# The first attention's TensorE order: written out by hand as a pipeline over heads, with the projections cut in three

## The chip, the cores and the metric

The kernel runs on one core of one Trainium2 chip. The metric is the device time of one execution, in microseconds. All weights are read from the chip's HBM during the run; the activations of the 256 tokens stay in the core's SBUF.

## What is computed

A trunk of two layers over 256 tokens of width 2048 (SEQ = 256, DEPTH = 2). Layer 0's token mixer is a sparse attention with 32 heads; only this part is touched by the change. Cut to what matters:

```python
def dsa_attention(h, w_in, ..., w_qb, w_idx_qb, w_uk, w_uv, w_out, rel_bias):
    q_lat, c_kv, k_idx, w_idx = jnp.split(h @ w_in, ...)         # 512, 256, 128, 16 columns, normalised
    q = (q_lat @ w_qb).reshape(B, S, 32, 128)
    ...
    score = jnp.einsum('bqsh,bqh->bqs', jax.nn.relu(dots), wb)   # 16 indexer heads
    _, idx = lax.top_k(score, 64)                                # which keys a token may see
    logits = (q . w_uk . kv_sel) * 128 ** -0.5 + rel_bias[bucket]
    probs = softmax(logits)
    out = (probs . kv_sel . w_uv)                                # 32 heads of 128
    return out @ w_out
```

The top 64 keys are expressed as a mask over all 256 keys. Layer 1's mixer is a stick-breaking attention, and each mixer is followed by an MLP of 8192 hidden columns; these stages follow the touched one and are the same in both kernels.

## The kernel before

**Split products.** Weights are fetched as fp32 (`raw`, 128x1024, a ring of 4 buffers, loads issued by SP in order) and each is split into a high part (`whi`, ScalarE, L128) and a low part (`wlo`, VectorE, L129), rings of 4 buffers each. A product is then three matmuls (high with high, high with low, low with high: `mm3` L123 to L125, `m_piece` L353 to L355).

**The first attention** works on groups of four heads, `hq` from 0 to 7. `a_project(hq)` makes the group's queries (`pqT`, 48 matmuls of 256 columns), keys (`pkT`, 24) and values (`pv`, 12 of 512 columns), from one unit of query weights (two `raw`) and one `raw` each for keys and values. `a_attend(hq, hl)` handles one head: logits `lg` (L776) with the mask added (L779); a softmax on VectorE (L784, L786, L791) and ScalarE (exp L789, scaling L794); three transposes `pT` (L797), which ScalarE copies to SBUF (L799); the values' product `av` (L802, L803); and a split of its result into `o`. `a_out(hq, d)` multiplies a group's four heads with one of four blocks of `a_w_out` (`m`, 24 matmuls of 512 columns), added into `y` on VectorE.

**The mask.** VectorE finds the 64 largest scores by eight rounds of maximum and replacement (L829, L830) for each half of the tokens, GpSimd cuts the causal part (L833), TensorE transposes the result (`mt`, L839).

**The filler.** At fixed points (`filler.tick`) VectorE adds rows of the conditioning weights (`adaw`, L205) for later stages; a finished gate is spread over the partitions by two small matmuls per quarter (`gate`, L244, L245), with a split `ahl` (L128, L129) in between.

**What sets the order.** The kernel is written as a program and a scheduler reorders the instructions of each engine by readiness and program order, with cost estimates of its own. So in the kernel before, TensorE's order in the attention is the scheduler's, made from this loop: 

```python
for hq in range(8):
    ready, projected = projected, a_project(hq + 1) if hq < 7 else None
    for hl in range(4):
        a_attend(hq, hl, *ready)
        if hq > 0:
            a_out(hq - 1, hl)
```

Each engine executes its own order strictly one after another, and an instruction that waits holds up all behind it.

Of the kernel before, what the change touches and what calls it, by code (L numbers as in the profile page):

```python
# [12 lines left out]
AF = mybir.ActivationFunctionType  # L13
# [3 lines left out]
P = 128  # L17
# [16 lines left out]
BLK = 512  # L34
NB = D // BLK
# [8 lines left out]
def trunk(ctx: ExitStack, tc: tile.TileContext, x, c, rel_bias, ada_w, ada_b, norm_g, a_w_in, a_q_norm,  # L44
          a_kv_norm, a_idx_k_norm, a_w_qb, a_w_idx_qb, a_w_uk, a_w_uv, a_w_out, b_w_in, b_w_out,
          mlp_w1, mlp_w2, bucket, out):
    nc = tc.nc
# [71 lines left out]
    def rows(w, k0, k1, c0, c1):  # L119
        return w.rearrange("(a p) n -> p a n", p=P)[:, k0:k1, c0:c1]  # L120
# [27 lines left out]
    def bank(kind, name):  # L148
        ring = rings[kind]
        ring[1] += 1  # L150
        return psum.tile([P, BLK], F32, tag=f"bank{ring[0][(ring[1] - 1) % len(ring[0])]}", name=uid(name))

    def small_ps(name, tag="s"):
        return bank(tag, name)
# [174 lines left out]
    def unit(src, a, n, weight=1, into=None):  # L329
        if prepared:  # L330
            return prepared.pop()
        r = halves(fetch(src, a, n), a, n, into)
        filler.tick(weight)
        return r
# [148 lines left out]
    def pair_tile(i, name):  # L483

        return arena.tile([P, 2, 2, T], F32R, tag=f"slot{i}", name=uid(name))
# [99 lines left out]
    outs = ((pq, BLK, 0), (pk, W2, BLK))  # L585
    waiting = []
    for i in range(len(steps) + LEAD):
        if i < len(steps):
            start_load(i)
            g, k, _ = steps[i]  # L590
# [134 lines left out]

    def a_project(hq):

        qparts = unit(rows(a_w_qb[0], 0, 4, hq * BLK, (hq + 1) * BLK), 4, BLK)
        khi, klo = a_kv_unit(uk_src, hq)
        vhi, vlo = a_kv_unit(uv_src, hq)  # L730
        qk = []
        for a in range(2):
            pf = bank("f", "pqT")
            s_piece([(k, hi[:, a * 2 * P:(a + 1) * 2 * P], lo[:, a * 2 * P:(a + 1) * 2 * P])
                     for k, (hi, lo) in enumerate(qparts)], q_of, 2, [pf], 4)
            qT = q_tile[:, hq % 2, a].rearrange("p (a t) -> p a t", a=2)
            nc.scalar.activation(qT, pf.rearrange("p (a t) -> p a t", a=2), AF.Copy, scale=QS)
            pf = bank("f", "pkT")
            for b in range(2):
                for k in range(2):  # L740
                    xh, xl = kv_of(k)
                    h = a * 2 + b
                    mm3(pf[:, b * T:(b + 1) * T], khi[:, h, k * P:(k + 1) * P], klo[:, h, k * P:(k + 1) * P],
                        xh, xl, start=(b == 0 and k == 0), stop=(k == 1))
            kT = k_tile[:, hq % 2, a].rearrange("p (a t) -> p a t", a=2)
            nc.scalar.activation(kT, pf.rearrange("p (a t) -> p a t", a=2), AF.Copy)
            qk.append((qT, kT))
        vt = []
        pv = [bank("m", "pv") for _ in range(NT)]
        vu = [(k, vhi[:, :, k * P:(k + 1) * P], vlo[:, :, k * P:(k + 1) * P]) for k in range(2)]  # L750
        m_piece(vu, kv_of, [p_.rearrange("p (h d) -> p h d", h=4) for p_ in pv], 2)
        for t in range(NT):
            v = v_tile[:, hq % 2, t]
            nc.scalar.activation(v, pv[t], AF.Copy)  # L754
            vt.append(v)
        return qk, vt

    biases, o_tile = {}, {}

    def a_attend(hq, hl, qk, vt):  # L760

        a, b = divmod(hl, 2)
        qT, kT = qk[a]
        if hl == 0:
            biases[0] = arena.tile([P, 2, 2, T], F32, tag=f"slot{12 + hq % 2}", name=uid("bias"))
        if b == 0:
            nc.gpsimd.dma_start(out=biases[0][:, a], in_=bass.AP(tensor=tab_d.tensor,
                                                                 offset=tab_d.offset + (4 * hq + hl) * 3 * P,
                                                                 ap=[[1, P], [3 * P, 2], [1, T]]))
            o_tile[0] = pair_tile((11, 16, 17, 18, 10)[(2 * hq + a) % 5], "o")  # L770
        bias = biases[0][:, a]
        ps = small_ps("lg", "lg")
        kw = dict(skip_group_check=True)
        for t in range(NT):
            f, ks = krng[t]
            nc.tensor.matmul(ps[:, f], qT[:, b, t * P:(t + 1) * P], kT[:, b, ks], start=(t == 0), stop=False, **kw)  # L776
        for i in range(3):
            f = slice(i * P, (i + 1) * P)
            nc.tensor.matmul(ps[:, f], mask_t[:, f], big_flip, start=False, stop=(i == 2), **kw)  # L779
        lg = lg_tile[:, hl % 2, :3 * P]  # L780
        st = small.tile([P, 6], F32, tag="st", name=uid("st"))
        for t in range(NT):
            f, _ = krng[t]
            nc.vector.tensor_tensor_reduce(lg[:, f], ps[:, f], bias[:, b, :(t + 1) * P], 1.0, -3.4e38,  # L784
                                           ALU.add, ALU.max, st[:, t:t + 1])
        nc.vector.tensor_scalar(st[:, 2:4], st[:, 0:2], -1.0, None, op0=ALU.mult)  # L786
        for t in range(NT):
            f, _ = krng[t]
            nc.scalar.activation(lg[:, f], lg[:, f], AF.Exp, bias=st[:, 2 + t:3 + t], accum_out=st[:, 4 + t:5 + t])  # L789
        rc = small.tile([P, 2], F32, tag="rc", name=uid("rc"))  # L790
        nc.vector.reciprocal(rc, st[:, 4:6])  # L791
        for t in range(NT):
            f, _ = krng[t]
            nc.scalar.activation(lg[:, f], lg[:, f], AF.Copy, scale=rc[:, t:t + 1])  # L794
        ps = small_ps("pT")
        for i, j in enumerate((0, 2, 1)):
            nc.tensor.transpose(ps[:, i * P:(i + 1) * P], lg[:, j * P:(j + 1) * P], ident)  # L797
        pT = pT_tile[:, hl % 2, :3 * P]
        nc.scalar.activation(pT, ps[:, :3 * P], AF.Copy)  # L799
        ps = small_ps("av", "av")  # L800
        hs = slice(hl * P, (hl + 1) * P)
        nc.tensor.matmul(ps[:, :T], vt[1][:, hs], pT[:, :T], start=True, stop=False, **kw)  # L802
        nc.tensor.matmul(ps[:, P:T], vt[0][:, hs], pT[:, T:], start=False, stop=True, **kw)  # L803
        o = o_tile[0][:, b]
        split(o[:, 0], o[:, 1], ps[:, :T])
        o_tiles[hq].append(o)
        filler.tick(0.33)

    def a_kv_unit(src, hq):
        raw = raw_tile()  # L810
        nc.sync.dma_start(out=raw.rearrange("p (h n) -> p h n", h=4), in_=src[:, 4 * hq:4 * hq + 4, :])
        hi, lo = part_tiles()
        split(hi, lo, raw)
        filler.tick(0.5)
        return hi.rearrange("p (h n) -> p h n", h=4), lo.rearrange("p (h n) -> p h n", h=4)
# [1 line left out]
    def o_of(tiles):  # L817
        return lambda k: (tiles[k][:, 0], tiles[k][:, 1])

    projected = a_project(0)  # L820

    for s in (slice(0, P), slice(2 * P, 3 * P)):
        nc.gpsimd.affine_select(out=score[:, s], in_=score[:, s], pattern=[[-1, P]], compare_op=ALU.is_ge,
# [22 lines left out]
        out_part(a_w_out[0], 4 * q, 4, o_of(o_tiles[q]), yt, gates.get((0, 2)), ss, d, q == 0, q == 7,  # L846
                 ("x", "f", "m")[-len(d):], **kw)

    for hq in range(8):
        ready, projected = projected, a_project(hq + 1) if hq < 7 else None  # L850
        for hl in range(4):
            a_attend(hq, hl, *ready)
            if hq > 0:
                a_out(hq - 1, hl)
    filler.finish()
    a_out(7, 0)
    early = {}
# [256 lines left out]
```

## Time and profile before

| what | value |
|---|---|
| median of 3 runs | 2447.61 us (2441.55 to 2448.34) |
| the profiled execution | 2444.33 us |
| its span, first to last instruction | 2442.5 us |
| TensorE (PE) busy | 2350.5 us, 96% |
| VectorE (DVE) busy | 1747.2 us, 72% |
| ScalarE (ACT) busy | 1222.3 us, 50% |
| mean granted TensorE clock | 0.988 |
| first q product of the attention, last `av` | 177.1 us, 508.99 us |

The difference between the execution's time and its span, 1.8 us, lies ahead of the first and behind the last instruction. Busy time of PE is the union of the records of its matmuls, whose ends are modelled; PEld are the weight loads, which overlap with matmuls. A released wait is shown as idle time and the name of what ended it.

### The profile page before, as it was taken

The page shows a single profiled execution, that of the slowest core. Times are in us where ns is not written, and L with a number is a line of the kernel's source. Part 1 is how long each engine was busy: PE and PEld are TensorE (multiplying, and loading weights), DVE is VectorE, ACT ScalarE, POOL GpSimd, SP SyncE. Part 2 cuts the span into 40 slices and gives each one's busy share as a digit, 9 for nine tenths or more (in the row PEclk, how much of TensorE's full clock was granted, in tenths as well). Part 3 has the DMA queues.
Part 4 walks back from the last instruction along what each step waited for, and adds up shares of the span by engine and source line. Part 5 has one row for each costly group of instructions (what it writes and reads, how often), then busy time and mean ns, then how long its engine had stood idle before and what let it go on. Part 6 is the DMA issues. An engine that isn't in the chain of part 4 may idle for free.

```text
span 2442.5 us, 32827 instructions
## 1 busy us (share of the span) xinstructions
PE 2350.5 (96%) x12292; PEld 1957.9 (80%) x12292; DVE 1747.2 (72%) x2218; ACT 1222.3 (50%) x1825; POOL 41.0 (2%) x74
## 2 busy tenths in 40 slices
PE   5789999999999999999999999999999999999998
PEld 2478887868888888888878989987788888888886
DVE  6789798888576876876567678887855557655556
ACT  3056555566544544444455554456654454454443
POOL 0010000000000000000000000000000000000000
PEclk9799999999999999999999999999999999999999
DMA  9986789857677877877657779896666557656554
GB/s 371 346 311 233 267 307 309 292 206 267 232 261 246 293 269 274 303 253 272 193 186 257 239 264 328 304 335 221 235 239 191 185 188 263 216 189 190 182 189 146
DMA packets 281831, 613.93 MB, mean 251 GB/s; under 512 B 19668, under 2 KB 36392, under 8 KB 281160
## 3 DMA queue, kind: packets, MB, share of 16 engines
q1 hardware_dynamic: 278544, 603.14, 71.8%
q0 software_dynamic: 2464, 8.53, 1.2%
q8 instruction: 96, 1.57, 0.3%
q14 instruction: 63, 0.52, 0.1%
q10 hardware_dynamic: 664, 0.17, 0.0%
HBM read 609.62 MB, written 2.15 MB: 250 GB/s over the span
## 4 chain that ended last, share of the span: by engine, by line
PE 78%; DMA 7%; DVE 5%; ACT 4%; issue 4%; POOL 0%; SPq 0%; DVEq 0%; POOLq 0%; ACTq 0%
PE f L884 18%; PE m L355 11%; PE m L354 11%; PE m L353 11%; PE f L886 9%; DVE acc L205 2%; DMA raw<-in_a_w_out_dram 2%; DMA w<-in_ada_w_dram 2%; DMA adaw<-in_ada_w_dram 1%; ACT whi L128 1%; PE pv L353 1%; PE pv L354 1%; PE pv L355 1%; DVE wlo L129 1%; PE pq L123 1%
## 5 line engine op out<-in xcount | busy, mean ns | idle before, releaser
L129 DVE TENSOR_TENSOR wlo<-raw,whi 128x1024 fp32r<-128x1024 f32 x726 | 875.5, 1220 | 424.6 <-ACT whi L128 421.5
L128 ACT ACTIVATE whi<-raw 128x1024 fp32r<-128x1024 f32 x726 | 756.0, 1056 | 806.9 <-PE f L884 311.2
L884 PE MATMUL f<-h,whi 128*128 128x512 f32 x1920 | 675.9, 394 | 0.0
L886 PE MATMUL f<-h,wlo 128*128 128x256 f32 x1920 | 543.2, 283 | 0.2 <-DVE wlo L129 0.2
L884 PEld LDWEIGHTS f<-h,whi 128*128 128x128 f32 x1920 | 360.6, 188 | 82.5
L205 DVE SCALAR_TENSOR_TENSOR acc<-adaw,cs,acc 128x1024 f32<-128x1024 f32 x300 | 384.1, 1280 | 53.1 <-DMA adaw<-in_ada_w_dram 49.8
L353 PE MATMUL m<-whi,hid 128*128 128x512 f32 x1016 | 401.4, 395 | 0.0
L355 PE MATMUL m<-wlo,hid 128*128 128x512 f32 x1016 | 400.9, 395 | 0.0
L354 PE MATMUL m<-whi,hid 128*128 128x512 f32 x1016 | 400.9, 395 | 0.0
L886 PEld LDWEIGHTS f<-h,wlo 128*128 128x128 f32 x1920 | 360.9, 188 | 1.9 <-DVE wlo L129 0.8
L355 PEld LDWEIGHTS m<-wlo,hid 128*128 128x128 f32 x1016 | 191.3, 188 | 44.7
L353 PEld LDWEIGHTS m<-whi,hid 128*128 128x128 f32 x1016 | 191.4, 188 | 44.0
L354 PEld LDWEIGHTS m<-whi,hid 128*128 128x128 f32 x1016 | 191.4, 188 | 43.3
L387 DVE TENSOR_TENSOR y<-m,y 128x512 f32<-128x512 f32 x200 | 136.7, 685 | 38.4 <-PE m L355 38.0
L353 PE MATMUL m<-whi,o 128*128 128x512 f32 x368 | 149.8, 407 | 0.0
L355 PE MATMUL m<-wlo,o 128*128 128x512 f32 x368 | 146.5, 400 | 0.4 <-DVE wlo L129 0.4
L354 PE MATMUL m<-whi,o 128*128 128x512 f32 x368 | 146.8, 399 | 0.0
L205 DVE SCALAR_TENSOR_TENSOR acc<-w,cs,acc 128x1024 f32<-128x1024 f32 (+1 forms) x74 | 79.6, 1075 | 11.1 <-DMA w<-in_ada_w_dram 8.9
L355 PEld LDWEIGHTS m<-wlo,o 128*128 128x128 f32 x368 | 69.4, 189 | 15.6 <-DVE wlo L129 1.0
L353 PEld LDWEIGHTS m<-whi,o 128*128 128x128 f32 x368 | 69.6, 189 | 13.6 <-ACT qkv L754 0.2
L354 PEld LDWEIGHTS m<-whi,o 128*128 128x128 f32 x368 | 69.6, 189 | 13.3
L123 PE MATMUL pk<-h,whi 128*128 128x256 f32 x256 | 72.8, 284 | 0.0
(274 smaller groups left out, 2912.9 us busy)
## 6 DMA issues: line engine op xcount, KB each, us to landing
raw<-in_mlp_w_dram SPq DMA_DIRECT2D x504, 512.0 KB, 4.5
adaw<-in_ada_w_dram SPq DMA_DIRECT2D x320, 512.0 KB, 6.3
raw<-in_b_w_in_dram SPq DMA_DIRECT2D x92, 512.0 KB, 5.2
raw<-in_a_w_out_dram SPq DMA_DIRECT2D x64, 512.0 KB, 5.6
w<-in_ada_w_dram SPq DMA_DIRECT2D x62, 512.0 KB, 10.3
raw<-in_b_w_out_dram SPq DMA_DIRECT2D x32, 512.0 KB, 6.9
raw<-in_a_w_qb_dram SPq DMA_DIRECT2D x16, 512.0 KB, 5.9
win<-in_a_w_in_dram SPq DMA_DIRECT2D x3, 1824.0 KB, 12.0
```

Of the source, the lines that this page charges most:

```text
L123: nc.tensor.matmul(o, sh, mh, start=start, stop=False, skip_group_check=True)
L128: return (nc.scalar.activation(dst_hi, src, AF.Copy).ins, nc.vector.tensor_sub(dst_lo, src, dst_hi.bitcast(F32)).ins)
L129: nc.vector.tensor_sub(dst_lo, src, dst_hi.bitcast(F32)).ins)
L205: nc.vector.scalar_tensor_tensor(acc, w, cs[:, k:k + 1], acc, op0=ALU.mult, op1=ALU.add)
L353: nc.tensor.matmul(o, xh[:, ts_], hi, start=(k == 0), stop=False)
L354: nc.tensor.matmul(o, xl[:, ts_], hi, start=False, stop=False)
L355: nc.tensor.matmul(o, xh[:, ts_], lo, start=False, stop=(k == n - 1))
L387: nc.vector.tensor_add(y, pt[d][t], y)
L884: nc.tensor.matmul(pf[f], hi[:, fs], hb.rearrange("p a t -> p (a t)"), start=(u == 0 and i == 0), stop=False, skip_group_check=True)
L886: nc.tensor.matmul(pf[f][:, :T], lo[:, fs], hb[:, 0], start=False, stop=(u == 3 and i == 3), skip_group_check=True)
```

## The change

`a_project` becomes a generator in three parts, queries, keys, values, and each part fetches and splits its weights only when it is reached (before, all splits of a group stood at its head, and queries and keys were made in two halves). `a_attend` becomes a generator in three parts: logits with softmax, transposes with their copy, `av` with the split. Around both, `tc.manual_schedule` for TensorE alone keeps TensorE's instructions in the order in which the program writes them; the other engines' orders are still the scheduler's. The new loop writes, for each step, the logits of one head, one `m` block of the group before, the transposes of the previous head, the next part of a projection, and the previous head's `av`. Every engine executes the same instructions as before, in another order.

```diff
     def a_project(hq):
 
-        qparts = unit(rows(a_w_qb[0], 0, 4, hq * BLK, (hq + 1) * BLK), 4, BLK)
+        both = lambda pf: pf.rearrange("p (a t) -> p a t", a=2)
+        qk, vt = ([], []), []
+        parts = unit(rows(a_w_qb[0], 0, 4, hq * BLK, (hq + 1) * BLK), 4, BLK)
+        pf = [bank("f", "pqT") for _ in range(2)]
+        s_piece([(k, hi, lo) for k, (hi, lo) in enumerate(parts)], q_of, 4, pf, 4)
+        for a in range(2):
+            qk[0].append(both(q_tile[:, hq % 2, a]))
+            nc.scalar.activation(qk[0][a], both(pf[a]), AF.Copy, scale=QS)
+        yield
         khi, klo = a_kv_unit(uk_src, hq)
-        vhi, vlo = a_kv_unit(uv_src, hq)
-        qk = []
         for a in range(2):
-            pf = bank("f", "pqT")
-            s_piece([(k, hi[:, a * 2 * P:(a + 1) * 2 * P], lo[:, a * 2 * P:(a + 1) * 2 * P])
-                     for k, (hi, lo) in enumerate(qparts)], q_of, 2, [pf], 4)
...
             pf = bank("f", "pkT")
...
+        yield
+        vhi, vlo = a_kv_unit(uv_src, hq)
         pv = [bank("m", "pv") for _ in range(NT)]
...
-        return qk, vt
+        projected[hq] = list(zip(*qk)), vt
...
-    def a_attend(hq, hl, qk, vt):
+    def a_attend(hq, hl):
+
+        qk, vt = projected[hq]
...
             nc.scalar.activation(lg[:, f], lg[:, f], AF.Copy, scale=rc[:, t:t + 1])
+        yield
         ps = small_ps("pT")
...
         nc.scalar.activation(pT, ps[:, :3 * P], AF.Copy)
+        yield
         ps = small_ps("av", "av")
...
-    projected = a_project(0)
+    projected = {}
+    attention_order = ExitStack()
+    attention_order.enter_context(tc.manual_schedule(engines={mybir.EngineType.PE}))
+    for _ in a_project(0):
+        pass
+    project = a_project(1)
+    next(project)
...
-    for hq in range(8):
-        ready, projected = projected, a_project(hq + 1) if hq < 7 else None
-        for hl in range(4):
-            a_attend(hq, hl, *ready)
-            if hq > 0:
-                a_out(hq - 1, hl)
+    heads = [divmod(h, 4) for h in range(32)]
+    outs = []
+    before = None
+    for hq, hl in heads + [(8, 0)]:
+        now = a_attend(hq, hl) if hq < 8 else None
+        if now:
+            next(now)
+        if outs:
+            a_out(*outs.pop(0))
+        if before:
+            next(before)
+        next(project, None)
+        if before:
+            next(before, None)
+        if hl == 0 and hq > 0:
+            outs += [(hq - 1, d) for d in range(NB)] if hq < 8 else []
+        if hl == 3:
+            for _ in project:
+                pass
+            project = a_project(hq + 2) if hq < 6 else iter(())
+        before = now
+    for o_ in outs:
+        a_out(*o_)
+    attention_order.close()
     filler.finish()
     a_out(7, 0)
```

The lines of the touched functions move: the transposes are L798 in the changed kernel and L797 before, their copy L800 and L799, `av` L804 and L805 for L802 and L803, `mt` L849 for L839, the maxima L839 for L829.

TensorE at the mask. In the kernel before, `mt` stands behind the projections of groups 0 and 1 (`pv_1463` is the last of group 1), the first logits of two heads and the first of group 2's keys (`pkT_1662`):

```order
L355 MATMUL pv_1463<-wlo_1372,ckv_638 128x512
L776 MATMUL lg_1481<-qkv_636,qkv_635 128x128
L776 MATMUL lg_1481<-qkv_636,qkv_635 128x256
L776 MATMUL lg_1514<-qkv_636,qkv_635 128x128
L776 MATMUL lg_1514<-qkv_636,qkv_635 128x256
L123 MATMUL pqT_1636<-qlat,whi_1607 128x256
...
L123 MATMUL pkT_1662<-ckv_638,whi_1620 128x256
L839 LDWEIGHTS misc
L839 MATMUL mt_1316<-ident_b,misc 128x128
```

In the changed kernel it stands right behind the queries of group 1 (`pqT_1281`), and the first head's logits, a gate and the keys of group 1 (`pkT_1441`) follow it:

```order
L123 MATMUL pqT_1281<-qlat,whi_1265 128x256
L124 MATMUL pqT_1281<-qlat,whi_1265 128x256
L125 MATMUL pqT_1281<-qlat,wlo_1266 128x256
L849 LDWEIGHTS misc
L849 MATMUL mt_1393<-ident_b,misc 128x128
...
L776 MATMUL lg_1410<-qkv_636,qkv_635 128x128
L776 MATMUL lg_1410<-qkv_636,qkv_635 128x256
L779 LDWEIGHTS misc
L779 MATMUL lg_1410<-big_flip,misc 128x128
...
L244 MATMUL gate_1434<-ahl_1277,ones_r 128x256
L245 MATMUL gate_1434<-ahl_1277,ones_r 128x256
L123 MATMUL pkT_1441<-ckv_638,whi_1428 128x256
```

Keys, values and the second group's first logits moved from ahead of the mask to behind it.

TensorE between a head's transposes and its `av`. Before, the transposes (`pT_2632`) are interleaved with an output block (`m_2661`) and the next head's logits (`lg_2688`):

```order
L797 MATMUL pT_2632<-ident,lg_640 128x128
L353 MATMUL m_2661<-whi_2650,o_2333 128x512
L797 MATMUL pT_2632<-ident,lg_640 128x128 x2
L354 MATMUL m_2661<-whi_2650,o_2333 128x512
L355 MATMUL m_2661<-wlo_2651,o_2333 128x512
L776 MATMUL lg_2688<-qkv_636,qkv_635 128x128
L802 MATMUL av_2637<-lg_641,qkv_637 128x256
```

In the changed kernel, in the last step of a group (here the third head of group 2, in the step of the fourth head's logits), an output block ends, the transposes follow it, and `av` follows them:

```order
L353 MATMUL m_2386<-whi_2375,o_1971 128x512
L354 MATMUL m_2386<-whi_2375,o_1971 128x512
L355 MATMUL m_2386<-wlo_2376,o_1971 128x512
L798 MATMUL pT_2413<-ident,lg_640 128x128 x3
L804 MATMUL av_2418<-lg_641,qkv_637 128x256
L805 MATMUL av_2418<-lg_641,qkv_637 128x128
L776 MATMUL lg_2426<-qkv_636,qkv_635 128x128
```

The products that stood between have moved ahead of the transposes. There are 13 such heads of 32.

ScalarE at the same place of the changed kernel (the waits as the program has them; `PE_49` is a wait for TensorE, `DMAHW` for a load):

```order
L794 ACTIVATE lg_640<-lg_640,rc_2363 128x128 [waits DVE_49]
L794 ACTIVATE lg_640<-lg_640,rc_2363 128x256 [waits Activation_49]
L128 ACTIVATE whi_2497<-raw_2493 128x1024 [waits DMAHW5_49,PE_49]
L128 ACTIVATE whi_2501<-raw_2494 128x1024 [waits DMAHW0_49,PE_49]
L800 ACTIVATE lg_641<-pT_2413 128x384 [waits PE_49]
L128 ACTIVATE o_2421<-av_2418 128x256 [waits PE_49]
```

The copy of the transposes stands behind two splits that wait for TensorE; `whi_2501` takes the fourth-last buffer in the ring of four, which is `whi_2375`, read by the output block above.

## Rows read from the trace of the kernel before

**Rows 1.** The page, part 1: busy time, share of the span, instructions.
```profile
PE 2350.5 (96%) x12292; PEld 1957.9 (80%) x12292; DVE 1747.2 (72%) x2218; ACT 1222.3 (50%) x1825; POOL 41.0 (2%) x74
```

**Rows 2.** Window: stretch, length, PE, PEld, DVE, ACT, POOL busy, PEclk, DMA share, GB/s.
```profile
209.00:512.00 303.00, 293.26 (x1630) 242.57 (x1629) 262.15 (x464) 183.43 (x385) 10.85 (x16) 0.99 0.84 287
```

**Rows 3.** Waits of PE, 209 to 512 us: total us, times, longest.
```profile
PE pT L797 <- ACT lg L794: 2.7, 5, 0.8
PE gate L244 <- ACT ahl L128: 2.6, 1, 2.6
PE av L802 <- ACT lg L799: 2.0, 4, 0.8
PE pkT L125 <- DVE wlo L129: 1.1, 1, 1.1
```

**Rows 4.** Timeline of PE (start, length): first `m` of a block, what follows its 24th.
```profile
361.16 0.48 PE L353 MATMUL m<-whi,o 128*128 128x512 f32 x1
...
366.82 0.27 PE L797 MATMUL pT<-ident,lg 128*128 128x128 f32 x1
```

**Rows 5.** Waits of the weight loads (PEld), 209 to 512 us.
```profile
PEld pT L797 <- ACT lg L794: 7.8, 16, 1.2
PEld av L802 <- ACT lg L799: 7.4, 20, 1.1
```

**Rows 6.** Timelines of DVE and PE around the mask.
```profile
182.95 0.28 DVE L829 MAX8 m<-misc 128x8 f32<-128x128 f32 x1
...
199.09 1.21 DVE L129 TENSOR_TENSOR wlo<-raw,whi 128x1024 fp32r<-128x1024 f32 x1
...
207.67 0.36 DVE L831 TENSOR_SCALAR misc<-misc 128x384 bf16<-128x384 f32 x1
...
208.44 0.53 PE L839 MATMUL mt<-ident_b,misc 128*128 128x128 bf16 x3 [1.79 <-POOL misc L833]
```

**Rows 7.** Timeline of PE: first of group 1's q products, and what follows the 24th.
```profile
190.18 0.28 PE L123 MATMUL pqT<-qlat,whi 128*128 128x256 f32 x1
...
193.02 0.28 PE L123 MATMUL pkT<-ckv,whi 128*128 128x256 f32 x1
```

**Rows 8.** Timeline: the copy of a head's transposes, its `av`.
```profile
373.77 0.49 ACT L799 ACTIVATE lg<-pT 128x384 f32<-128x384 f32 x1 [0.53 <-PE pT L797]
...
374.32 0.48 PE L802 MATMUL av<-lg,qkv 128*128 128x256 f32 x1
```

**Rows 9.** Timeline: last transposes, a split, their copy and `av` of another head.
```profile
427.86 0.44 PE L797 MATMUL pT<-ident,lg 128*128 128x128 f32 x2
...
428.69 1.06 ACT L128 ACTIVATE whi<-raw 128x1024 fp32r<-128x1024 f32 x1 [0.88 <-DMA raw<-in_a_w_qb_dram]
...
429.65 0.47 ACT L799 ACTIVATE lg<-pT 128x384 f32<-128x384 f32 x1
...
430.18 0.70 PE L802 MATMUL av<-lg,qkv 128*128 128x256 f32 x2 [0.53 <-ACT lg L799]
```

**Rows 10.** Timeline: a head's last logits, and the scaling that ends its softmax.
```profile
295.65 0.33 PE L779 MATMUL lg<-big_flip,misc 128*128 128x128 bf16 x3
...
299.18 0.80 ACT L794 ACTIVATE lg<-lg,rc 128x128 f32<-128x128 f32 x2 [0.28 <-DVE rc L791]
```

**Rows 11.** Timelines of ACT and DVE: the split between two gate products.
```profile
210.14 0.41 ACT L128 ACTIVATE ahl<-acc 128x256 fp32r<-128x256 f32 x1
...
210.59 0.42 DVE L129 TENSOR_TENSOR ahl<-acc,ahl 128x256 fp32r<-128x256 f32 x1
```

**Rows 12.** PE's timeline at the gate's wait; then windows as in rows 2.
```profile
261.54 0.39 PE L244 MATMUL gate<-ahl,ones_r 128*128 128x256 f32 x1 [2.58 <-ACT ahl L128]
...
262.60:266.00 3.40, 3.40 (x18) 3.31 (x17) 1.63 (x5) 1.32 (x3) 0.00 (x0) 0.50 1.01 389
...
126.00:132.80 6.80, 5.01 (x6) 2.19 (x7) 4.21 (x7) 3.69 (x6) 0.22 (x1) 0.50 0.58 199
...
547.00:560.00 13.00, 12.87 (x52) 7.40 (x53) 9.53 (x18) 12.53 (x25) 0.00 (x0) 1.00 0.18 55
```

More of the change, by code (lines that the diff above doesn't have):

```diff
@@ L726, in a_project @@
     def a_project(hq):
-        qparts = unit(rows(a_w_qb[0], 0, 4, hq * BLK, (hq + 1) * BLK), 4, BLK)
+        both = lambda pf: pf.rearrange("p (a t) -> p a t", a=2)
[7 more added lines that the diff above has]
+        yield
         khi, klo = a_kv_unit(uk_src, hq)
-        vhi, vlo = a_kv_unit(uv_src, hq)
-        qk = []
         for a in range(2):
-            pf = bank("f", "pqT")
-            s_piece([(k, hi[:, a * 2 * P:(a + 1) * 2 * P], lo[:, a * 2 * P:(a + 1) * 2 * P])
-                     for k, (hi, lo) in enumerate(qparts)], q_of, 2, [pf], 4)
-            qT = q_tile[:, hq % 2, a].rearrange("p (a t) -> p a t", a=2)
-            nc.scalar.activation(qT, pf.rearrange("p (a t) -> p a t", a=2), AF.Copy, scale=QS)
             pf = bank("f", "pkT")
@@ L744, in a_project @@
                         xh, xl, start=(b == 0 and k == 0), stop=(k == 1))
[L745 to L748, printed above, removed]
+            qk[1].append(both(k_tile[:, hq % 2, a]))
+            nc.scalar.activation(qk[1][a], both(pf), AF.Copy)
+        yield
+        vhi, vlo = a_kv_unit(uv_src, hq)
         pv = [bank("m", "pv") for _ in range(NT)]
@@ L752, in a_project @@
         for t in range(NT):
-            v = v_tile[:, hq % 2, t]
-            nc.scalar.activation(v, pv[t], AF.Copy)
-            vt.append(v)
-        return qk, vt
+            vt.append(v_tile[:, hq % 2, t])
+            nc.scalar.activation(vt[t], pv[t], AF.Copy)
+        projected[hq] = list(zip(*qk)), vt
     biases, o_tile = {}, {}
-    def a_attend(hq, hl, qk, vt):
+    def a_attend(hq, hl):
+        qk, vt = projected[hq]
         a, b = divmod(hl, 2)
@@ L769, in a_attend @@
                                                                  ap=[[1, P], [3 * P, 2], [1, T]]))
-            o_tile[0] = pair_tile((11, 16, 17, 18, 10)[(2 * hq + a) % 5], "o")
         bias = biases[0][:, a]
@@ L803, in a_attend @@
         nc.tensor.matmul(ps[:, P:T], vt[0][:, hs], pT[:, T:], start=False, stop=True, **kw)
+        if b == 0:
+            o_tile[0] = pair_tile((11, 16, 17, 18, 10)[(2 * hq + a) % 5], "o")
         o = o_tile[0][:, b]
```

## The prediction

> **What bounds the kernel now.** I read the page first: TensorE is busy for 96% of the span, VectorE for 72%, ScalarE for 50% [rows 1]. Then the window of the first attention, from the permuted mask at 208.4 to 512 us, where the last head's products end: TensorE is busy 293.26 of 303 us, VectorE 262.15, and the DMA engines at 0.84 [rows 2]. TensorE is the tightest there, so a microsecond in which it stands still is a microsecond of the span, unless its own later waits shrink. Third, who TensorE waits for in that stretch: 9.74 us in 14 places, 11 of them in the rows: transposes waiting for the softmax's scaling, a gate product, `av` waiting for the copy of the transposes, and a split [rows 2, 3]. That is all that a better order can win here. Each such wait costs some 0.16 us more than its idle time, because a record runs past the engine's next issue (an `m` record lasts about 0.4 us, but 24 of them follow each other in 5.66 us, 0.236 apart [rows 4]), so 9.74 + 14 × 0.16 = 12.0 us.
>
> The weight loads tell another number: they wait 7.8 us at the transposes and 7.4 us at `av` [rows 5], where the matmul records show 2.7 and 2.0. The Trainium skill (Perfetto Trace Analysis, Identifying the Most-Contended Engine) calls matmul busy time a poor measure of headroom and prefers the weight loads. By the loads the sum below would come out 15.2 − 4.7 = 10.5 us lower. I stay with the records: a weight load also "waits" while the matmul before it still streams, and the 0.16 us are in. The 10.5 us are kept as a bound.
>
> **1. The mask: 9.5 us lost.** Before the mask, the earlier order did both projections of groups 0 and 1, two heads' logits and most of the first part of group 2; only then did `mt` stand, waiting 1.79 us for GpSimd's last step of the mask [rows 6]. Now group 0's projection and the q part of group 1 (48 products) stand ahead of `mt`, and everything behind it in TensorE's queue, the k and v parts of group 1 included, waits with it. When does TensorE arrive? The first q product of group 1 started at 190.18 and 24 of them took 2.84 us [rows 7]; 48 end near 195.9. When is the mask ready? VectorE works from its first maximum at 182.95 to 207.67 without a gap worth naming [rows 6]; its new order has the same maxima and replacements, and six splits instead of eight in between. Two splits of 1.21 us [rows 6] saved bring 208.4 to 206.0 at best; if the rounds, each waiting for the one before, show their own delay where splits covered it, nothing is saved. So TensorE waits 10.1 to 12.5 us where it waited 1.8: +8.3 to +10.7, I take +9.5. What could cover it is the 11 us of products that now stand behind; nothing else is left to do. ScalarE's and VectorE's splits run on until all four `whi`/`wlo` pairs are taken, then they and SP's loads stand too.
>
> **2. Transposes with `av` right behind: 15.7 us lost.** A head's `av` needs ScalarE's copy of its transposes. In three of four heads a part of a projection now stands between (2.8 to 5.7 us, ample). In 13 heads nothing does: two in group 0, the third head of groups 1 to 6, all four of 7 and the fourth of 6 (the project generator is spent). The shortest path in the trace: the copy, released by the transposes, runs from 373.77 for 0.49 and `av` starts at 374.32, 0.55 us; with the 0.16 us of record past issue, 0.7 [rows 8]. That is the lower price, 13 × 0.7 = 9.1. But in 11 of the 13 ScalarE's queue has a pair of `whi` splits just ahead of the copy, and the second of them overwrites the buffer that the `m` products just before the transposes read last. It starts when they end and takes 1.06 us, then the copy 0.47 [rows 9]; the three transposes cover 0.3. That is 1.25 to 1.5 us each. The trace has one such case: the transposes ended at 428.30, `whi` ran from 428.69, `av` came at 430.18, 1.88 us [rows 9]; there `lg` and `m` products filled most of it. I take 11 × 1.3 + 2 × 0.7 = 15.7; the upper end, with the 1.88 and its 0.16 less the transposes' own 0.3, is 11 × 1.7 + 1.4 = 20. Behind the waiting `av` stand the next head's logits and the next `m`.
>
> **3. Group 0's softmax: 3 us lost.** From group 1 on, a head's logits precede its transposes by 24 `m` products and more, twice over: over 11 us [rows 4], against the quickest softmax in the trace, 4.0 us (295.98 to 299.98) [rows 10]; nothing waits. In group 0 no `m` exists yet. Between the logits of heads 2 and 3 and their transposes stand 2 to 3 us of products; with 4.0 needed, one to two us are missing twice. I take 3, from 1 to 6 (filler sums of 1.2 us stand in VectorE's queue between its softmax steps).
>
> **4. Gates and splits: 2.5 us.** Two gate products of one gate are now adjacent; the second needs a ScalarE step of 0.41 and a VectorE step of 0.42 after the first [rows 11] with two hand-overs: 1.0 us, from 0 to 2.6. For splits that come late I put 1.5, near the 1.1 shown [rows 3]; below 0, because each split now has a step's lead; above 5, if VectorE's queue holds one behind a softmax step. Loads cost nothing: SP issues the same loads, the k and v ones a step or two later, and the DMA engines have room (0.84) [rows 2].
>
> **5. The clock: 2.5 us.** The gate's wait of 2.58 us ended at 261.54, and the granted clock was 0.50 (1.2 of 2.4 GHz) from 262.6 to 266.0, 1.7 of 3.4 us lost; after waits of the next stage, from 547 on, it stayed at 1.00. Ahead of the attention, where TensorE was busy for 5.0 of 6.8 us, it stood at 0.50 for all of them [rows 12]. A wait of 11 us at the mask should lower it: 1.7 to 3.4 us lost after; I take 2.5.
>
> **Sum**: 9.5 + 15.7 + 3 + 2.5 + 2.5 = 33.2, less 12.0 of old waits and 1.7 of old half clock (13.7): +19.5, rounded down to +19 us (0.8%). The profiled execution took 2444.33 us, a span of 2442.5 and 1.8 around it: 2463.3. The median of the three runs is 3.3 us above it; on that base 2466.6. I forecast **2465**, from a base of 2446 between the two. The lower ends give 8.3 + 9.1 + 1 + 0 + 1.7 − 13.7 = +6.4, with the weight loads' 10.5 us taken off as well −4.1; the upper ends 10.7 + 20 + 6 + 7.6 + 3.4 − 13.7 = +34.
>
> **Rivals.** *The head start pays (not slower).* While TensorE stands at the mask, the split buffers and loads fill, and if that lead lasts, no split, softmax or gate is late again. Every old wait goes, counted by the weight loads, and `av` costs its lower price: −4.1 us, **2442**. It decides if ScalarE's copy starts within 0.1 us of the transposes in the 13 heads. For it: VectorE and the DMA are nearly as full as TensorE [rows 2], so their lead is worth something. Against: only four buffers of each kind exist, filled within one step, and the `whi` pair in ScalarE's queue is a fixed order. 0.2, of which 0.07 gains over 0.3%.
> *The clock stays low.* Waits of 1.3 us and more now recur in every group; the clock fell after a wait of 2.58 us [rows 12], and none of the rest, 0.8 us at most but for one of 1.1 [rows 3], lowered it. If it falls at eight of them and after the mask for 6.8 us: 8 × 1.7 + 3.4 − 2.5 = 14.5 more, **2479**. It decides where the granted clock shows under 0.97 over the attention. The skill (TensorE: Matmul & The Clock Gate, HAM oscillation) has idle gaps return the array to its lower clock, and keeps matmul bursts close together for that; the trace agrees at 262.6 and not at 547. 0.13.
> *Splits bind.* VectorE had 41 us to spare in 303 [rows 2]. If its queue puts a split behind each head's softmax steps, one split of 1.2 us is late in 28 steps: +34, **2499**. It decides if TensorE waits for `wlo` in most steps. Against it: the order puts most of a step's splits ahead of that step's logits. 0.05.
> Something else that makes the stretch faster, 0.02; my forecast (2454 to 2475) 0.6.
>
> **Numbers.** About 0.3%, 7 us, is what a measurement of this kernel can tell from no change. Slower: 0.6 + 0.13 + 0.05 = 0.78; within: 0.13 of the first rival; faster: 0.07 + 0.02 = 0.09. The range of 8 in 10 runs from 2449, inside the first rival, to 2483, past the second.
>
> **What would show it.** After: `mt` starts near 208 with 10 to 12 us of idle before it, on GpSimd's mask; `av` waits for ScalarE's copy some 13 times at 1 to 1.5 us; transposes wait for the scaling only in group 0; a half clock near 205 to 212; the attention ends near 531 instead of 512; from there to the end all is as before. Wrong would be: a mask ready before 204; `av` waits under 10 us in all; or later stages that differ.

## The result and the profile after

| | before | changed |
|---|---|---|
| median of 5 runs each | 2446.2 us (2441.55 to 2448.34) | 2466.65 us (2464.19 to 2467.92) |
| profiled execution, span | 2444.33 us, 2442.5 us | 2467.92 us, 2465.9 us |
| first `hT` behind the attention starts | 536.19 us | 559.52 us |

The changed kernel takes 1.0085 times as long, 95% interval 1.0073 to 1.0098, some 21 us more. All of it lies in the first attention: its end moves by 23.3 us, and from the first `hT` to the end of the span both take 1906 us.

The windows of the changed kernel, in the columns of [rows 2]: from the start of the attention to `mt`, from there to the last `av`, the two stretches at half clock, and the whole attention up to the first `hT`:

```profile
176.00:206.76 30.76, 19.60 (x146) 18.50 (x145) 29.48 (x72) 13.88 (x21) 2.05 (x4) 0.89 0.69 235
206.76:536.70 329.94, 305.00 (x1713) 256.96 (x1713) 269.32 (x472) 189.44 (x394) 11.06 (x17) 0.99 0.79 272
206.80:210.20 3.40, 3.40 (x16) 2.89 (x17) 1.41 (x8) 0.42 (x1) 0.15 (x1) 0.50 0.00 0
227.40:230.80 3.40, 3.40 (x15) 2.86 (x15) 2.35 (x6) 1.19 (x3) 1.03 (x2) 0.50 0.92 242
...
176.00:559.52 383.52, 346.57 (x1954) 293.02 (x1952) 315.88 (x571) 215.10 (x442) 14.23 (x22) 0.98 0.76 260
```

In the kernel before, the whole attention (176 to 536.19 us) holds 347.81 us of busy TensorE in 360.19. So its idle time grew from 12.4 to 36.9 us, by 24.6, while its busy time is 1.2 us shorter. The time went into waits. Who TensorE waits for, from 176 to 559 us of the changed kernel (total us, times, longest):

```profile
PE av L804 <- ACT lg L800: 12.4, 11, 1.7
PE mt L849 <- POOL misc L843: 11.2, 1, 11.2
PE pT L798 <- ACT lg L794: 2.4, 1, 2.4
PE col L215 <- DVE mod L216: 2.3, 2, 1.2
PE col L215 <- ACT lg L800: 1.9, 2, 1.0
PE gate L244 <- ACT lg L800: 1.7, 2, 1.0
PE av L804 <- DVE o L129: 1.3, 1, 1.3
PE gate L244 <- DVE gg L246: 1.3, 1, 1.3
PE m L354 <- DVE o L129: 0.8, 1, 0.8
PE pv L353 <- ACT y L385: 0.8, 1, 0.8
```

Beside [rows 3, 6]: the mask's wait is 11.2 where it was 1.79, the copy of the transposes is waited for eleven times instead of four, and the filler's products (`gate`, `col`), which had one wait, now have seven, 7.2 us. The old waits for the scaling (five times, 2.7 us) are gone but for one in group 0.

One of the eleven, in the timeline of all engines of the changed kernel:

```profile
357.92 1.06 ACT L128 ACTIVATE whi<-raw 128x1024 fp32r<-128x1024 f32 x1 [0.33 <-PE m L354]
357.96 0.49 PE L798 MATMUL pT<-ident,lg 128*128 128x128 f32 x3
...
358.89 0.47 ACT L800 ACTIVATE lg<-pT 128x384 f32<-128x384 f32 x1
...
359.41 0.48 PE L804 MATMUL av<-lg,qkv 128*128 128x256 f32 x1 [0.96 <-ACT lg L800]
```

The split on ScalarE is released by the last `m` product that read its buffer, 0.04 us before the transposes start. It holds ScalarE for about a microsecond, the copy follows, and `av` after that: 0.96 us of idle. Where the wait is longer, 1.2 to 1.7 us (five places), another step of ScalarE stands in that queue too, the scaling of the next head's softmax or the copy of an output block. The longest, from the timelines of ACT and PE:

```profile
444.76 1.06 ACT L128 ACTIVATE whi<-raw 128x1024 fp32r<-128x1024 f32 x1 [0.38 <-PE m L354]
445.73 0.78 ACT L794 ACTIVATE lg<-lg,rc 128x128 f32<-128x128 f32 x2
446.42 0.47 ACT L800 ACTIVATE lg<-pT 128x384 f32<-128x384 f32 x1
...
446.94 0.70 PE L804 MATMUL av<-lg,qkv 128*128 128x256 f32 x2 [1.70 <-ACT lg L800]
```

### The profile page after: what moved, and what is told of

It reads as the page before. It is cut to its first block, busy times and chain, and to the rows that moved or that the text cites. A ratio compares the mean times of both kernels' runs of the same rounds, so it can differ in the third digit from the quotient of the medians.

```text
span 2465.9 us, 32836 instructions
## 1 busy us (share of the span) xinstructions
PE 2348.7 (95%) x12292; PEld 1960.7 (80%) x12292; DVE 1749.5 (71%) x2218; ACT 1222.2 (50%) x1825; POOL 40.7 (2%) x74
## 4 chain that ended last, share of the span: by engine, by line
PE 79%; DMA 6%; ACT 5%; DVE 5%; issue 4%; POOL 0%; SPq 0%; DVEq 0%; POOLq 0%; ACTq 0%
PE f L913 17%; PE m L353 12%; PE m L354 12%; PE m L355 12%; PE f L915 9%; DMA adaw<-in_ada_w_dram 3%; DMA w<-in_ada_w_dram 2%; DVE acc L205 2%; ACT whi L128 2%; PE pv L353 1%; PE pv L354 1%; DVE wlo L129 1%; PE pv L355 1%; PE pk L124 1%; PE pk L125 1%
## 5 line engine op out<-in xcount | busy, mean ns | idle before, releaser
L205 DVE SCALAR_TENSOR_TENSOR acc<-w,cs,acc 128x1024 f32<-128x1024 f32 (+1 forms) x74 | 79.6, 1075 | 11.2 <-DMA w<-in_ada_w_dram 9.0
L123 PE MATMUL pq<-h,whi 128*128 128x256 f32 x256 | 72.9, 285 | 0.0
```

The source lines that it names most:

```text
L123: nc.tensor.matmul(o, sh, mh, start=start, stop=False, skip_group_check=True)
L205: nc.vector.scalar_tensor_tensor(acc, w, cs[:, k:k + 1], acc, op0=ALU.mult, op1=ALU.add)
```

## The experiments

All are edits of the changed kernel. Ratios are to the kernel before, in the same series; the changed kernel's is 1.0085. The runs of the kernel before had medians of 2442.6 to 2446.2 us in these series, so versions are compared by their ratios first. The stages behind the attention took 1903 to 1910 us in the profiled executions, with the same program there, so where the attention ends is a second measure, with less noise from elsewhere.

### The same program without the hand-written order

```diff
-    attention_order.enter_context(tc.manual_schedule(engines={mybir.EngineType.PE}))
```

> The changed kernel without the hand-written order: the three-part projection, the generators and the new loop stay, and TensorE's order is the scheduler's again. Theory (the loss is the order's): the mask's wait is back near 2 us, since the scheduler puts the keys, values and the second group's queries ahead of it, the `av` waits are a few of 0.5 us, and the time is that of the kernel before, 2446, within 4 us. Rival (the rewriting makes the loss, above all weights split when due): at least half of the 20 us stays, 2456 or more, as waits for `wlo`.

Measured: 2433.01 us, 0.9945 times the kernel before (0.9927 to 0.9962). Neither theory nor rival: the time is not that of the kernel before, it is 13 us less. Its waits of TensorE from 176 to 521 us, where its attention ends, all of them:

```profile
PE mt L848 <- POOL misc L842: 2.3, 1, 2.3
PE gate L244 <- DVE st L786: 1.4, 1, 1.4
PE av L804 <- ACT lg L800: 0.8, 1, 0.8
PE pT L798 <- ACT lg L794: 0.2, 1, 0.2
```

So the change is two changes of opposite sign: the rewritten program is worth about −13 us (0.9945), and TensorE's order by hand costs 1.0085 / 0.9945 = 1.0141, some +34 us. In the profiled executions the attention ends at 521.3 us, 15 us sooner than before and 38 us sooner than with the order by hand. At the mask the scheduler puts group 1's keys and values, two heads' first logits and 37 products of group 2's queries ahead of `mt`, which waits 2.3 us. Three experiments ask for the gain, the others for the loss.

### Where the gain comes from

Splits at the head of the projection again, in the scheduler's order:

```diff
         parts = unit(rows(a_w_qb[0], 0, 4, hq * BLK, (hq + 1) * BLK), 4, BLK)
+        khi, klo = a_kv_unit(uk_src, hq)
+        vhi, vlo = a_kv_unit(uv_src, hq)
...
         yield
-        khi, klo = a_kv_unit(uk_src, hq)
...
         yield
-        vhi, vlo = a_kv_unit(uv_src, hq)
```

> The version with the new program and the scheduler's order (2433.0 us), with one thing put back: a group's key and value weights are fetched and split at the head of its projection, beside the query weights, as in the kernel before. Theory (the ring of four: split all at once, a projection takes every `whi` and `wlo` buffer and the output block's splits and the softmax's ScalarE steps queue behind): half or more of the 13 us comes back, 2440 to 2446, as waits of the transposes for the scaling and of products for `wlo`. Rival (the gain is the new loop's: logits a step ahead): stays at 2433, within 3 us.

Measured: 2432.16 us, 0.9945 (0.9928 to 0.9961). The theory of the ring falls: splitting when due is worth nothing that can be measured.

The old loop, with the projection in three parts and the scheduler's order:

```diff
-    for hq, hl in heads + [(8, 0)]:
...
+    for hq in range(8):
+        if 0 < hq < 7:
+            for _ in a_project(hq + 1):
+                pass
+        for hl in range(4):
+            for _ in a_attend(hq, hl):
+                pass
+            if hq > 0:
+                a_out(hq - 1, hl)
```

> The counterpart: three-part projection with splits when due, the scheduler's order, but the loop of the kernel before (a whole projection at a group's head, then for each head its logits, transposes and `av` together and one output block). Theory of the ring: the gain stays, 2433 to 2437. Rival (the gain is the new loop's): back near 2446, 2442 or more.

Measured: 2442.98 us, 0.9997 (0.9987 to 1.0006), the time of the kernel before. The gain is the new loop's. It writes a head's logits a step ahead of its transposes and the projection's parts between; which of the two makes the gain isn't separated. With the old loop the first of TensorE's waits is the old one, as in [rows 3]:

```profile
PE pT L798 <- ACT lg L794: 2.4, 4, 1.2
```

### The mask and group 0

The order by hand only from the sixth head on:

```diff
-    attention_order.enter_context(tc.manual_schedule(engines={mybir.EngineType.PE}))
...
+        if (hq, hl) == (1, 1):
+            attention_order.enter_context(tc.manual_schedule(engines={mybir.EngineType.PE}))
```

> The changed kernel, with the hand-written order of TensorE taken up only from the logits of the sixth head on; the mask, all of group 0 and the first head of group 1 are in the scheduler's order. Theory (the sum of uncovered places): the mask's wait goes from 11.2 to about 2.3 us, the softmax wait of 2.4, two `av` waits and one of the half-clock stretches of group 0 go too, 14 to 16 us less than the changed kernel, 2451 to 2453; the ten `av` waits of groups 1 to 7 stay. Rival (the head start at the mask is worth something: splits and loads fill while TensorE waits): the later waits grow, and less than 9 us is won, 2458 or more.

Measured: 2456.32 us, 1.0040 (1.0027 to 1.0053): 0.0045 of 2446, 11 us less than the changed kernel; in the profiled execution the attention ends 13.1 us sooner. From 176 to 546 us:

```profile
PE av L804 <- ACT lg L800: 12.5, 12, 1.7
PE col L215 <- DVE mod L216: 2.3, 2, 1.2
PE mt L848 <- POOL misc L842: 2.1, 1, 2.1
```

The mask's wait is 2.1 us where it was 11.2, and the later `av` waits are as they were. The time won is a little under what was expected; 11 us is over the rival's 9, but with some 4 us either way doesn't exclude it, and the rows, 13.1 us without longer waits later, do.

The mask sooner, with TensorE's order untouched:

```diff
-        for _ in range(TOPK // 8):
+        for _ in range(TOPK // 16):
```

> The changed kernel with four rounds of maximum and replacement instead of eight for each half of the tokens: it leaves out half of the search, so the mask holds the 32 largest scores. TensorE's order is the same; VectorE's 23.8 us between the first maximum and the mask hold 16.6 us of rounds beside six splits, so the mask comes about 8 us sooner. Theory (TensorE's wait at the mask is lost time): the wait falls from 11.2 to about 3 us and the time by 8 to 9 us, 2457 to 2459. Rival (the splits and loads that fill meanwhile pay for part of it): the later waits grow and less than 5 us is won, 2462 or more.

Measured: 2460.61 us, 1.0073 (1.0058 to 1.0088). The mask came at 199.8 instead of 206.8 us and its wait fell to 4.5:

```profile
PE mt L849 <- POOL misc L843: 4.5, 1, 4.5
```

In the profiled executions the attention ends 7.5 us sooner and the span is 8.7 us shorter. By the ratios the gain is 3 us, and their intervals together allow −2 to 8; beside the two versions below, timed in the same series, it is 10. The rows speak for the theory, but the size isn't settled by the time, which lies between the two expected ranges. And part of the rival shows: at the fifth head's `av` this version was 9.9 us ahead, then the `av` of group 1's third head waited 2.95 us instead of 1.46, and the clock fell at 520.2, where it had not.

Keys and values ahead of the mask:

```diff
     project = a_project(1)
-    next(project)
+    for _ in project:
+        pass
```

> The changed kernel with the keys and values of group 1 (36 products, about 6 us) written ahead of the mask instead of into the steps of group 0. Theory (the work that covers the mask is taken from group 0, whose softmax and copies it covered): the mask's wait falls by 6 us to about 5, and 4 to 6 us of it come back as waits of group 0's transposes for the scaling and of its `av` for the copy: 2462 to 2466. Rival (group 0's waits overlap, and its products are free to move): 2460 or less.

Measured: 2470.71 us, 1.0111 (1.0095 to 1.0126). No gain, as the theory had it, but not by its path alone. The mask came 2.7 us later (209.5), VectorE having two more splits among the rounds, so its wait fell by 3.2 us only. In group 0 the bare `av` waits and the scaling take some back, and the granted clock stood at 0.50 from the mask's wait through nearly all of group 0 (columns as in [rows 2]):

```profile
204.30:221.20 16.90, 9.46 (x36) 6.75 (x36) 8.76 (x37) 4.92 (x16) 0.54 (x2) 0.50 0.17 54
```

At the fifth head's `av` it was still 3.6 us ahead of the changed kernel; the attention ended 0.7 us behind it, after two more stretches at 0.50.

Work in the mask's wait:

```diff
+    warm = small_ps("warm")
+    for i in range(84):
+        nc.tensor.matmul(warm[:, :T], ones_r, q_of(i % 4)[0], start=True, stop=True)
     ps = small_ps("mt").bitcast(BF16)
```

> The changed kernel with 84 more products of 256 columns into the mask's PSUM tile, ahead of `mt`, that nobody reads: about 10 us of work in the wait of 11.2. Theory (the half clock after the mask comes from TensorE's idling there): the granted clock stays at 1.00 through the mask and the 3.4 us behind it, the 1.6 to 1.8 us lost there are won, 2465, which the rows show and the time can't. Rival (it falls for another reason): 0.50 behind the mask as before.

Measured: 2470.39 us, 1.0108 (1.0089 to 1.0126). The first window is the one behind the mask, the second lies later (columns as in [rows 2]):

```profile
206.80:210.20 3.40, 3.39 (x30) 3.23 (x30) 1.79 (x9) 1.49 (x6) 0.00 (x0) 1.00 0.00 0
264.90:268.20 3.30, 3.30 (x14) 2.64 (x13) 1.24 (x6) 0.74 (x3) 0.00 (x0) 0.50 0.88 319
```

The theory holds for the place: with TensorE busy through the wait but for its last microsecond, the clock behind the mask was 1.00, and 30 products started in a window that had held 16. The changed kernel's second stretch, at 227.4, went as well; at the fifth head this version is 4.5 us ahead. But the clock then fell at 264.8 and at 527.6, where it had not, single `av` waits grew (to 2.6 us), and the attention ends at 559.3, where it did. What was won at the clock did not last.

Part of the loss can be followed. The `av` of group 1's third head, in this version (first three lines) and in the changed kernel (last two):

```profile
251.80 1.28 DVE L205 SCALAR_TENSOR_TENSOR acc<-adaw,cs,acc 128x1024 f32<-128x1024 f32 x1 [1.15 <-DMA adaw<-in_ada_w_dram]
...
259.25 0.40 ACT L789 ACTIVATE lg<-lg,st 128x128 f32<-128x128 f32 x1 [2.96 <-DVE st L786]
...
264.21 0.70 PE L804 MATMUL av<-lg,qkv 128*128 128x256 f32 x2 [2.55 <-ACT lg L800]
...
263.16 0.40 ACT L789 ACTIVATE lg<-lg,st 128x128 f32<-128x128 f32 x1 [1.63 <-DVE st L786]
...
268.35 0.70 PE L804 MATMUL av<-lg,qkv 128*128 128x256 f32 x2 [1.46 <-ACT lg L800]
```

TensorE came to these transposes 5.2 us ahead of the changed kernel. VectorE, after a wait for one of the filler's loads, reached the next head's softmax with less of a lead: that head's exp, which stands ahead of the copy in ScalarE's queue, came 3.9 us ahead. So 1.1 us went into the wait and about 1.6 into the half clock behind it. With half the search and with the keys and values ahead of the mask the same `av` waited 2.95 and 3.19 us, VectorE having waited 1.56 and 1.79 us for the same kind of load (0.94 in the changed kernel). That the load is the cause isn't shown by a run.

### Transposes, their copy and `av`

The transposes ahead of the output block:

```diff
-        if outs:
-            a_out(*outs.pop(0))
         if before:
             next(before)
+        if outs:
+            a_out(*outs.pop(0))
```

> Starting from the changed kernel (2466.65 us), the previous head's transposes are written ahead of the step's output block instead of behind it, so 24 `m` products (5.7 us) stand between transposes and `av` in every step that has a block. Theory (the sum of uncovered places): the ten `av` waits of groups 1 to 7 (0.96 to 1.70 us idle each, about 1.3 from start to start) vanish, the two of group 0 stay, the mask's wait stays at 11: 13 us less, 2453 to 2455, about 1.003 times the kernel before. Rival (the stretch is held by VectorE's splits and the loads): what is saved at `av` comes back as waits for `wlo` or a load, and the time stays within 3 us of 2466.

Measured: 2459.99 us, 1.0056 (1.0038 to 1.0073); the profiled attention ends 10.8 us sooner. The ten `av` waits are gone, but part of them is back under other names:

```profile
PE col L215 <- ACT lg L800: 2.8, 4, 1.1
...
PE pT L798 <- DVE mod L216: 1.3, 1, 1.3
...
PE pT L798 <- DVE gg L246: 1.0, 1, 1.0
```

`col`, `gate` and `pT` take turns in one PSUM bank. A filler product behind the transposes waits for their copy, and transposes behind a filler product wait until VectorE has read that: 8.5 us in all beside the 7.2 of the changed kernel. TensorE's idle time falls by 11.5 us, from 36.1 to 24.6, and two more stretches at half clock (282.4 and 350.7, 3.4 us each) give back 3.4. So the theory's 13 is 11 at the attention's end; the time shows 7, with some 5 either way.

Splits behind the copy:

```diff
+    copied = []
+
     def split(dst_hi, dst_lo, src):
-        return (nc.scalar.activation(dst_hi, src, AF.Copy).ins,
-                nc.vector.tensor_sub(dst_lo, src, dst_hi.bitcast(F32)).ins)
+        with tc.issue_after(copied[0]) if copied else nullcontext():
+            hi = nc.scalar.activation(dst_hi, src, AF.Copy).ins
+        return hi, nc.vector.tensor_sub(dst_lo, src, dst_hi.bitcast(F32)).ins
...
-        nc.scalar.activation(pT, ps[:, :3 * P], AF.Copy)
+        copied[:] = [nc.scalar.activation(pT, ps[:, :3 * P], AF.Copy).ins]
```

> Starting from the changed kernel, each weight split on ScalarE is queued behind the latest copy of transposes that the program has reached, so that no split stands ahead of a copy that TensorE waits for. TensorE's order is the same. Theory (the splits ahead of the copy make up about half of each `av` wait): the waits of groups 1 to 7 fall from 0.96 to 1.70 us to about 0.55 each, 5 to 6 us less, about 2461, 1.006 times the kernel before. Rival (the copy and the hand-overs alone make the wait): the waits stay at 0.96 and the time at 2466. Second rival: splits now come late, `m` waits for `wlo`, and the time rises above 2468.

Measured: 2545.36 us, 1.0397 (1.0370 to 1.0424). From 209 to 640 us:

```profile
PE m L358 <- DVE wlo L132: 10.0, 9, 3.6
PE pv L356 <- ACT whi L131: 9.7, 7, 1.7
PE pqT L123 <- ACT whi L131: 8.1, 6, 1.7
PE pkT L123 <- ACT whi L131: 7.2, 6, 1.9
PE av L807 <- ACT lg L803: 7.1, 12, 0.7
```

The last row is the theory's: without a split ahead, `av` waits 0.59 us each, where it waited 1.13. The other rows are the second rival's, far above its 2468: each split now starts only when a step's transposes are through, and the products that need it wait instead. The splits ahead of the copy are what keeps TensorE supplied; the copy can't simply be put first.

Another bank for the filler's products:

```diff
-        ps = small_ps("col")
+        ps = small_ps("col", "lg" if "lg" in rings else "s")
...
-        ps = small_ps("gate")[:, :T]
+        ps = small_ps("gate", "lg" if "lg" in rings else "s")[:, :T]
```

> Starting from the changed kernel, the filler's small products (`gate`, `col`) take their PSUM tile from the two banks of the logits instead of the one bank that the transposes use too. Theory (a filler product right behind the transposes waits for their copy because it needs their bank): the four waits of `gate` and `col` on the copy, 0.7 to 1.0 us each, about 4 us in all, go, and the waits of adjacent products of one gate or column set (1.3, 1.2 and 1.1 us) go down where only the bank held them: 2460 to 2463. Rival (they wait for their own splits and sums): 2466, with the same waits under another name.

Measured: 2459.91 us, 1.0059 (1.0043 to 1.0075), about 6 us less; the profiled attention ends 10.1 us sooner. What is left of the filler's waits:

```profile
PE col L215 <- DVE mod L216: 1.2, 1, 1.2
...
PE gate L245 <- DVE ahl L129: 0.6, 1, 0.6
PE gate L244 <- ACT ahl L128: 0.6, 1, 0.6
```

2.4 us in place of 7.2, and none for the copy. The bank held them. All waits together fall further, from 36.1 to 27.7 us; in this version the `av` waits (10.8 us) and others came out shorter too, which the edit doesn't explain.

### Repaired, and the fastest

Transposes ahead of the block, the filler in the logits' banks and the order by hand from the sixth head on (the three edits above, together):

> Three repairs of the hand-written order together: taken up from the sixth head on, the transposes ahead of the output block, and the filler's small products in the logits' banks. Apart, the second and the third each took some 7 us off the changed kernel. Theory: no uncovered place is left but the filler's own; 2432 to 2438, level with the scheduler's order of the same program (2433.0), 0.994 to 0.997 times the kernel before. Rival (an order by hand can't follow the splits' and loads' times as the scheduler does): 2443 or more.

Measured: 2435.47 us, 0.9960 (0.9947 to 0.9973). The transposes ahead of the block and the other bank together take 1.0040 / 0.9960, some 20 us, off the version that has only the late start; apart they took 7 and 6 by the time. In the profiled attention it is 17.3 us, beside 10.8 and 10.1, so they add up but for a few microseconds. The order by hand is then level with the scheduler's, not ahead of it.

The new program in the scheduler's order, with the filler in the logits' banks:

> The new program in the scheduler's order (2433.0 us) with the filler's small products in the logits' banks. Theory: there only one gate product waits (1.4 us) and none for the copy, so it changes nothing, 2431 to 2435. Rival (the bank holds the scheduler's order too): 2430 or less.

Measured: 2429.34 us, 0.9940 (0.9925 to 0.9956), against 0.9945 without; the profiled attention ends at 519.9 instead of 521.3 us. In microseconds that is inside the rival's range, but the kernel before was 3.3 us faster in this series; by the ratios the difference is 1 us with some 6 either way. It is the fastest version here, and the other bank's worth in it isn't clear of the noise.

## Why the prediction was right, by its steps

The forecast was 2465, a loss of 19; measured 2466.65. Its gross loss of 33.2 us and its credit of 13.7 can be set beside runs that have one without the other: the order by hand costs about 34, and the rewritten program alone gives about 13. The mechanism was right in its main terms; that the total came out within 2 us is in part luck, as the steps show.

| step | forecast, us | found in the profile, us |
|---|---|---|
| 1, the mask | +9.5 | 11.16 − 1.79 = +9.4 idle |
| 2, `av` behind its transposes | +15.7 | 12.4 + 1.3 idle in 12 places, with 0.16 each 15.6 |
| 3, group 0's softmax | +3 | 2.4 idle, once |
| 4, gates and splits | +2.5 | 7.2 at `gate` and `col`, 0.8 at `pv`, 0.8 at `m` |
| 5, the clock | +2.5 | two stretches of 3.4 us at half rate, 3.4 |
| old waits and old half clock | −13.7 | −13 by the program alone |

*The mask* came at 206.76, within the forecast 206.0 to 208.4, and TensorE stood from 195.6. That this is lost time, and no head start, is shown by the version with the order by hand from the sixth head on (0.0045 less) and by the rows of the one with half the search; the price of the mask alone rests on the rows.

*`av`* waited in 12 places, not 13 (behind the last head's transposes stand output products), and for the reason given, late splits ahead of the copy, with one addition: in five places the next head's scaling or an output block's copy stands there too. With the splits behind the copy the wait fell to the bare path, 0.59 us beside the 0.55 of [rows 8]. One of the 12, in group 0, was ended by VectorE's split of the result before, since all `av` share one bank; that wasn't foreseen.

*Step 4 was mis-sized*, by some 6 us. It counted two gate products that now follow each other, but not that the transposes' PSUM bank is also the filler's: a filler product right behind transposes waits for their copy. The version with the filler in another bank shows it.

*The sum of the steps* with the measured terms put in is 9.4 + 15.6 + 2.4 + 8.8 + 3.4 − 13.7 = 25.9 (a gross of 39.6 for the 33.2 forecast), where the attention grew by 23.3 and the time by 21. The waits and the clock would have lengthened TensorE's busy time too, yet it is 1.2 us shorter. From start to start in the timeline, an `m` product followed by a transpose took 0.265 us before (39 places) and 0.233 in the changed kernel (28), about 1 us in all; such changes between kinds of product were not in the forecast, and no experiment takes them apart. That such terms made up for part of step 4's error is luck.

*One sign* was off: the last `av` was to end near 531 instead of 512 us, and it starts at 536.70 instead of 508.99, 27.7 us later. From there to the first `hT` the changed kernel takes 22.8 us instead of 27.2, which the forecast didn't foresee either.

*The credit* was right in size, but the prediction let it go with TensorE's new order. It belongs to the new loop: with the old loop it is lost, with the splits at the projection's head it stays. The first rival, a head start that pays, fails: most of the old waits did go, but without the mask's wait they go too, in the scheduler's order, so the 9.4 us bought nothing. The second, a low clock throughout, fails too: the mean granted clock is 0.99 from the mask on. Of the third, splits that bind, nothing shows in the changed kernel; the splits queued behind the copy show what it would look like.

Open are the size of the mask term in the time alone, what makes the gain in the new loop, and why the clock fell at new places when a gain was made ahead of 250 us (half the search, keys and values ahead of the mask, work in its wait), so that part or all of it was not kept to the end of the attention.

## What to carry to other kernels

A change that rewrites a program and fixes an order is two changes: run it with the order left to the scheduler before judging either. When writing an engine's order by hand, look in each step for a result that must pass through another engine before the next instruction can start, and put work of more than that engine's whole queue between (here 5.7 us of products between transposes and `av`); count every product that shares their PSUM bank as standing in that place too. Putting the other engine's urgent piece first isn't the same: it moved the splits behind the transposes and made the time 1.0397 instead of 1.0085 times the kernel before, some 76 us more.

## What the hardware showed that was not expected

The granted clock's falls did not follow the length of one wait. In the changed kernel it fell after a wait of 2.44 us (ahead of 225.51), and in the version with work in the mask's wait after one of 2.55 (ahead of 264.21); a wait of 1.70 (ahead of 446.94, changed kernel) left it at 1.00. So far the longer waits lowered it. But in the version with half the search a longer wait, 2.95 us, left it at 1.00:

```profile
259.13 0.70 PE L804 MATMUL av<-lg,qkv 128*128 128x256 f32 x2 [2.95 <-ACT lg L800]
...
259.20:262.60 3.40, 3.40 (x19) 2.89 (x20) 1.70 (x7) 1.18 (x4) 0.00 (x0) 1.00 0.89 287
```

And in the version with the transposes ahead of the block it fell at 350.7, where two waits of 1.29 and 0.58 us stand within 1.1 us, neither of which lowers it alone elsewhere. The `av` of the last head but one and the filler product behind it wait 0.97 and 1.09 us in the changed kernel, which stays at 1.00, and 0.96 and 1.09 with the keys and values ahead of the mask, where it falls at 528.5. The prediction had read from one kernel that waits of about a microsecond are safe. And versions that lost one stretch at half clock often got another, 1.7 us each, so a term for the clock is better read from several executions than from one.
